# Turning an FFN's hidden features with transposing transfers of 16-bit halves in place of TensorE transposes

## Chip, cores and metric

One Trainium2 chip, one of its cores. The metric is device time in microseconds (us) for one execution of the whole program. TensorE (PE) multiplies, VectorE (DVE) and ScalarE (ACT) do elementwise work, GpSimd (POOL) here mostly issues accumulating transfers, and SyncE (SP) issues nearly all other transfers.

## The reference, cut to what matters

Float32 throughout, 512 tokens of width 1024. The change lies in the two feed-forward networks (FFN) of the block, which have 2816 hidden features each:

```python
def swiglu(h, w1, w3, w2):
    return (jax.nn.silu(h @ w1) * (h @ w3)) @ w2

x = x + 0.5 * swiglu(rms_norm(x, ffn1_norm[l]), ffn1_w1[l], ffn1_w3[l], ffn1_w2[l])
...                       # two token mixers, merged by gates, and an output projection
x = x + 0.5 * swiglu(rms_norm(x, ffn2_norm[l]), ffn2_w1[l], ffn2_w3[l], ffn2_w2[l])
return rms_norm(x, final_norm)
```

## The kernel before, in words

A float32 product is made of three TensorE products: each operand is split into a high part (a copy on ScalarE) and a low part (a subtraction on VectorE), and `mm3` multiplies high by high, high by low and low by high.

Each FFN runs in three stages. The first 256 hidden features are made in a plain way. The other 2560 are five *wide blocks* of 512 features (class `Wide`, L650). A block is computed with seven products (n = 0 to 6) instead of eight, a Strassen-like scheme over two token halves and two halves of the depth. One product is 24 matmuls of 128x128 by 128x512. The last stage (class `Seven`, `run`, L570 on) multiplies the hidden features by `w2`, again with seven products.

`s.order` (L666 to 670) lists the (block, product) pairs, 35 in all; `blocks` (L898 on) walks it, and `m` is the place in the list. In the middle of the walk, block b-1 is not finished when block b begins: the list reads (b,0), (b-1,3), (b-1,4), (b,1), (b,2), (b,6), (b,5). During product m the weights of product m+2 are split into a ring of four slots, one half when the first 12 matmuls of m are done and one when the other 12 are (`weight`, L705). Behind each split, `weight` issues the next transfer into the buffer it read: plain loads from SP (`plain`, L688), accumulating ones from POOL (`add`, L692). `finish` (L801) takes a product's sum out of PSUM.

A block's result lies in `u`: `u[0]` holds tokens 0 to 255 and is ready after product 4, where VectorE multiplies it by the gate `p`; `u[1]` holds tokens 256 to 511 and is ready after product 3, where it is multiplied by the gate `sa`. Each is 128 tokens x 2 x 512 features. The last stage needs features on the partitions, so the block is turned. `turn_all` (L793) does it for blocks 0 to 3: for each of four 128-feature groups, four 128x128 transposes on TensorE (against `ident`) into one PSUM bank, and one ScalarE copy of 128x512 into `s.seven.hidden(j)`, which are the tiles `rl` and `rh`. Block 4 is turned by `turn` (L783), which is another function.

Inside `blocks`, VectorE, ScalarE and TensorE run in the order in which the code is written (class `Queued`, L92). The order on SP is chosen by the framework's scheduler. ScalarE works through its row in order, so an instruction that waits holds up all casts behind it.

Before the second FFN, `tokens` (L1083) already turns eight other tiles with transposing transfers: ScalarE takes the two 16-bit halves of each float32 apart, SP issues a transfer with `transpose=True` (L1087), and POOL joins the halves (L1089).

Of the kernel before, what the change touches and what calls it, by code (L numbers as in the profile page):

```python
# [12 lines left out]
U16 = mybir.dt.uint16  # L13
# [6 lines left out]
P = 128  # L20
# [62 lines left out]
def kernel(  # L83
# [6 lines left out]
    nc = tc.nc  # L90
# [17 lines left out]
    dve, act, pe = [Queued(e, False) for e in (nc.vector, nc.scalar, nc.tensor)]  # L108
# [22 lines left out]
    ident = cp.tile([P, P], F32, name="ident")  # L131
# [368 lines left out]
    KH, TH, LO, HI = KF // 2, T // 2, slice(0, D // 2), slice(D // 2, D)  # L500

    BLOCKS, EARLY = (KF - 2) // 4, 2
# [147 lines left out]
    class Wide:  # L650


        def __init__(s, hp, kind, nrm, w1, w3, w2, quads, residual, C=None):
            def four(name):
                return [hp.tile([P, 2, T], F32, name=f"{name}{h}")[:] for h in range(2)]

            s.nrm, s.w, s.x, s.residual, s.later = nrm, (w1, w3), quads, residual, ()
            s.seven = sv = kind(hp, w2)
            s.A, s.B, s.C = [four("ca"), four("cd")], four("cb"), C or four("cc")
            s.extra = hp.tile([P, 2, T], F32R, name="extra")  # L660
            s.u = [hp.tile([P, 2, T], F32, name=f"u{i}")[:] for i in range(2)]
            q = [hp.tile([P, 2, 4, TH], F32R, name=f"q{i}") for i in range(3)]
            s.q = {n: (t[:, 0], t[:, 1]) for n, t in zip((1, 4, 3), q)}
            s.small = [hp.tile([P, NB], F32, name=f"sm{n}") for n in range(5)]
            s.end = BLOCKS - 1
            s.order = [(b, n) for n in (0, 6) for b in range(EARLY)]  # L666
            s.order += [(0, 1), (0, 2), (0, 4), (0, 5), (1, 1), (0, 3), (1, 2), (1, 4), (1, 5)]
            for b in range(EARLY, BLOCKS):
                s.order += [(b, 0), (b - 1, 3), (b - 1, 4)][:3 if b > EARLY else 2] + [(b, n) for n in (1, 2, 6, 5)]
            s.order += [(s.end, 4), (s.end, 3)]  # L670
            sv.parts = kind.PARTED
            e, o = [t[:].rearrange("p a t -> p (a t)").rearrange("p (b d) -> p b d", b=2) for t in quads]
            flat = [t.rearrange("p a t -> p (a t)") for t in (*s.C, *s.u)]
            sv.wide, sv.fg = s, flat[2]
            sv.O = [o[:, 0], o[:, 1], flat[0], flat[1]]
            sv.e = [t.rearrange("p (k t) -> p k t", t=TH) for t in (e[:, 0], e[:, 1], flat[3][:, 0:3 * TH])]
            a1, a0 = s.chain(s.end - 1), s.chain(s.end)
            sv.sum = [*a1, *s.B, a0[0], a0[1][:, 0:1]]
# [111 lines left out]
                cols = slice(half * TH, (half + 1) * TH)  # L790
                act.copy(s.seven.hidden(2 + 4 * s.end + f)[:, cols], s.turns[f][:, cols])

        def turn_all(s, b, fs):  # L793
            for f in fs:
                ps = s.Y[b % 2][f % 2]
                for i in range(4):
                    pe.transpose(ps[:, i * P:(i + 1) * P], s.u[i // 2][:, i % 2, f * P:(f + 1) * P], ident[:])
            for f in fs:
                act.copy(s.seven.hidden(2 + 4 * b + f), s.Y[b % 2][f % 2][:])

        def finish(s, m):  # L801
            b, n = s.order[m]
# [95 lines left out]
        def blocks(s, pa, pb, more):  # L898
            sv, end, nrm = s.seven, s.end, s.nrm
            raw = [[t[k][:, 0:TH] for k in range(KD)] for t in (nrm.hi, nrm.lo)]  # L900
            soon = {(0, 0): ((s.sums, 1),), (0, 6): ((s.low, 1),), (1, 6): ((s.low, 2),), (0, 1): ((s.low, 4),),
                    (0, 2): ((s.low, 5),), (0, 5): ((s.low, 3),)}
            todo = {(0, 0): ((s.gated, 0),),
                    (1, 0): ((s.cast, 1), (s.sums, 2)),
                    (0, 6): ((s.cast, 2), (s.sums, 4), (s.back, 0)),
                    (1, 6): ((s.cast, 4), (s.sums, 5), (s.hidden, 1, pa[:], pb[:])),
                    (0, 1): ((s.cast, 5), (s.gated, 1)),
                    (0, 2): ((s.cast, 3),),
                    (0, 5): ((s.cast, 0),),
                    (0, 3): ((s.low, 0), (s.cast, 6)),  # L910
                    (1, 2): ((s.low, 6), *[(s.plain, sv.O[i], s.residual[i]) for i in range(2)]),
                    (2, 5): ((sv.second, 0),), (3, 2): ((sv.two, 0),),
                    (end, 0): ((sv.operand, 0, 0),), (end, 2): ((sv.operand, 0, 1),), (end, 6): ((sv.one, 0),),
                    (end, 5): ((sv.second, 1), (sv.one, 1)), (end, 4): ((sv.two, 1),)}
            for at, steps in more.items():
                todo[at] = tuple(todo.get(at, ())) + steps
            for m, (b, n) in enumerate(s.order):
                apart = n == 4 and (b < EARLY or b == end)
                early = m < 2 * EARLY
                ps = s.X[b % 2] if n in (0, 2, 3, 5) or early else s.X[(b + 1) % 2] if n == 6 or apart else s.Y[b % 2]  # L920
                onto = n in (2, 3, 5) or (n == 6 and early) or (n == 4 and not apart)
                last = m + 2 >= len(s.order)
                if last:
                    sv.slots += s.ring[2 * m % 4:2 * m % 4 + 2]
                for h in range(2):
                    wh, wl = s.ring[(2 * m + h) % 4]
                    for i in range(2):
                        for k in range(2):
                            c = slice(i * P, (i + 1) * P)
                            if early:  # L930
                                qh, ql = [t[4 * (n > 0) + 2 * h + k][:, c] for t in raw]
                            else:
                                qh, ql = [t[:, 2 * h + k, c] for t in s.q[n]]
                            mm3(ps[i][:], qh, ql, wh[:, k], wl[:, k], not onto and h + k == 0, h + k == 2, onto)
                    if b > 1 and (n, h) == (2, 0):
                        s.turn_all(b - 1, (2, 3))
                    if (b, n) == (1, 2):
                        s.turn_all(0, ((0, 1), (2, 3))[h])
                    if h == 1:
                        if m == len(s.order) - 1:  # L940
                            s.turns = dict(zip((0, 2, 1, 3), s.Y[end % 2] + s.X[1 - end % 2]))
                            act.activation(s.sa[0], ps[0][:], AF.Silu)
                            act.activation(s.sa[1], ps[1][:], AF.Silu)
                            s.turn((0, 2), 0)
                            for i in range(2):
                                dve.tensor_tensor(s.u[1][:, i], s.u[1][:, i], s.sa[i], op=ALU.mult)
                            sv.operand(0, 2)
                        else:
                            s.finish(m)
                        if b > 1 and n == 1:  # L950
                            s.turn_all(b - 1, (0, 1))
                    if h == 1:
                        for f, *a in soon.get((b, n), ()):
                            f(*a)
                    if not last:
                        s.weight(m + 2, h)
                    elif len(sv.slots) == 2:
                        sv.weight(0, h)
                    elif h == 0:
                        sv.slots.insert(2, s.last)  # L960
                        sv.weight(0, 2)
                        sv.weight(0, 3)
                    else:
                        sv.weight(0, 4)
                s.gate(m)
                for f, *a in todo.get((b, n), ()):
                    f(*a)
            sv.slots.append(tuple(tmp("g5", (P, 1, T), F32R)[:] for _ in range(2)))
            sv.junk = [tmp(f"osq{i}")[:] for i in range(2)]
            sv.weight(0, 5)  # L970
            sv.run()
# [121 lines left out]
    with ExitStack() as mx:  # L1093
# [102 lines left out]
        for o, c0, mu in ((spare[2], DA, 4), (spare[3], 0, 0)):  # L1196
            ps = bank("pk", pf)
# [3 lines left out]
        for p in range(NP):  # L1201
            za.append((zslots[2 * p], zslots[2 * p + 1]))
            for i, (w_, x_, par0, o) in enumerate(((uw, lw, PAR_W0, zslots[2 * p]), (ux, lx, PAR_A0, zslots[2 * p + 1]))):
                ps = bank("pz", (pr, pf)[i])
# [181 lines left out]
        for t in range(C - 1):  # L1386
            n, m = t + 1, C - 1 - t
# [103 lines left out]
        at = b1.go(range(2))  # L1491
# [9 lines left out]
        at = b1.go(range(2, 5), a0.sum(at))  # L1501
# [3 lines left out]
        at = b1.go(range(5, 7), b0.sum(at))  # L1505
# [16 lines left out]
        at = ahead.go(range(7))  # L1522
# [254 lines left out]
        sees, turned, exps, copies, yb = [], ([], []), [], [], []  # L1777
# [176 lines left out]
        ycs, sqs, pgs, pus, parts = [None] * NP, [None] * NP, [None] * NP, [None] * NP, {}  # L1954
# [70 lines left out]
        ps = proj(0, fox_proj, ybs, fws[0])  # L2025
        for m in range(KD):
# [11 lines left out]
            if m + 1 < KD:  # L2038
                ps = proj(m + 1, fox_proj, ybs, fws[m + 1])
# [29 lines left out]
        for m in range(KD):  # L2069
            g = slot[m]  # L2070
            ps = proj(m, rwkv_proj, ya)
# [136 lines left out]
```

## Time and profile before

| what | value |
|---|---|
| median of 3 runs | 1082.54 us (1082.31 to 1082.6) |
| the profiled execution's own time | 1083.12 us |
| its span | 1081.3 us |
| granted TensorE clock | 0.999 |
| instructions | 16859 |

The profile has a page (busy time of each engine, 40 slices of the span, the chain that ended last, groups of instructions) and views on its trace: a timeline of single instructions, busy times in chosen stretches, and waits. A row of the timeline gives start, duration, engine, line, operation, output <- inputs, and in brackets the idle time before it with what ended it. Matmuls overlap: a matmul of 128x512 has a duration of 0.39 us, and the next one starts 0.23 us later, so the pace on TensorE is read from starts, not from durations. Line L103 is the recording helper through which most instructions of the FFN go, so there the names of the tiles tell them apart. The names are: `P` a PSUM bank; `swhi`, `swlo`, `sraw`, `extra` the ring of split weights; `ca`, `cb`, `cc`, `cd` the buffers in which weights land; `u`, `p`, `sa` as above. In this profile, the wide blocks of the first FFN run until about 231 us, those of the second from about 770 to 968 us.

### The profile page before, as it was taken

How to read it: one execution, taken by the hardware profiler on the slowest of the kernel's cores; microseconds unless marked ns; L12 is line 12 of the kernel's file. 1: busy time of each engine (PE TensorE's matmuls, PEld its weight loads, DVE VectorE, ACT ScalarE, POOL GpSimd, SP SyncE). 2: the span in 40 equal slices, each digit the busy share in tenths (PEclk: the TensorE clock that was granted, in tenths of full speed). 3: DMA queues.
4: the chain of work that ended last, by engine and by line, in shares of the span. 5: the costliest groups of instructions: out<-in, count | busy, mean ns of one | idle time of the engine just before them, and what ended most of it. 6: DMA issues, size and time to landing. Idle time of an engine off the chain costs nothing.

```text
span 1081.3 us, 16859 instructions
## 1 busy us (share of the span) xinstructions
PE 1072.1 (99%) x6346; PEld 881.2 (81%) x6346; DVE 829.7 (77%) x1155; ACT 677.4 (63%) x1063; POOL 223.9 (21%) x275
## 2 busy tenths in 40 slices
PE   9999999999999999999999999999999999999997
PEld 7888888888887887888878887888888888888886
DVE  7998575789865698888777777866697666699874
ACT  6775556576555666445888876545576555576554
POOL 1221120134202302412000120125321212114210
PEclk9999999999999999999999999999999999999999
DMA  7989978769955443444312244677977979869972
GB/s 209 261 174 229 217 164 207 180 150 187 233 138 167 110 115 95 128 136 118 89 46 81 91 133 148 192 161 205 290 156 178 211 197 188 194 147 203 235 189 78
DMA packets 150543, 179.23 MB, mean 166 GB/s; under 512 B 20542, under 2 KB 86654, under 8 KB 150462
## 3 DMA queue, kind: packets, MB, share of 16 engines
q0 software_dynamic: 33392, 70.14, 33.8%
q1 hardware_dynamic: 116334, 106.58, 33.1%
q10 hardware_dynamic: 736, 1.45, 0.3%
q8 instruction: 50, 0.82, 0.3%
q14 instruction: 31, 0.25, 0.1%
HBM read 163.51 MB, written 12.52 MB: 163 GB/s over the span
## 4 chain that ended last, share of the span: by engine, by line
PE 96%; DVE 2%; ACT 1%; issue 1%; DMA 0%; ACTq 0%; DVEq 0%
PE P L103 40%; PE P L176 6%; PE P L175 6%; PE P L177 6%; PE pgt L103 5%; PE l L103 3%; PE spot L103 3%; PE pq L103 3%; PE ppj L103 2%; PE pk L177 2%; PE pk L175 2%; PE pk L176 2%; PE pw L176 1%; PE pw L177 1%; PE pw L175 1%; PE f L103 1%
## 5 line engine op out<-in xcount | busy, mean ns | idle before, releaser
L103 PE MATMUL P<-sraw,q 128*128 128x512 f32 x344 | 91.3, 389 | 0.0
L103 PEld LDWEIGHTS P<-sraw,q 128*128 128x128 f32 x344 | 64.6, 188 | 13.4
L103 PE MATMUL P<-swhi,q 128*128 128x512 f32 x224 | 71.4, 390 | 0.0
L103 PE MATMUL P<-sraw,wxh 128*128 128x512 f32 x200 | 68.4, 394 | 0.0
L167 ACT CAST whi<-raw 128x1024 fp32r<-128x1024 f32 (+2 forms) x42 | 40.4, 961 | 43.3 <-issue 14.2
L103 PE MATMUL P<-swhi,wxh 128*128 128x512 f32 x144 | 56.9, 395 | 0.0
L103 PE MATMUL P<-swhi,wxl 128*128 128x512 f32 x144 | 56.1, 390 | 0.0
L103 PE MATMUL P<-swlo,wxh 128*128 128x512 f32 x144 | 56.1, 389 | 0.0
L168 DVE TENSOR_TENSOR wlo<-raw,whi 128x1024 fp32r<-128x1024 f32 (+2 forms) x43 | 48.5, 1127 | 9.4 <-ACT whi L167 8.3
L693 POOL DMA_DIRECT2D cd<-in_ffn_w_dram x24 | 29.5, 1229 | 119.2 <-DVE swlo L103 38.3
L693 POOL DMA_DIRECT2D cb<-in_ffn_w_dram x20 | 24.1, 1207 | 144.7 <-DVE cd L103 80.0
L103 PE MATMUL P<-sraw,wxl 128*128 128x512 f32 x136 | 53.0, 390 | 0.0
L103 PEld LDWEIGHTS P<-swhi,q 128*128 128x128 f32 x224 | 42.1, 188 | 8.7
L103 PE MATMUL P<-swlo,q 128*128 128x512 f32 x112 | 43.6, 389 | 0.0
L103 ACT CAST sraw<-cd 128x1024 fp32r<-128x1024 f32 x30 | 31.5, 1050 | 19.0 <-PE P L103 11.5
L103 ACT COPY RD<-spot 32x128 f32<-32x128 f32 (+2 forms) x128 | 39.9, 311 | 5.3 <-PE spot L103 2.3
L103 PEld LDWEIGHTS P<-sraw,wxh 128*128 128x128 f32 x200 | 37.2, 188 | 7.3
L552 POOL DMA_DIRECT2D ca<-in_ffn_w_dram x16 | 19.3, 1205 | 95.8 <-DVE swlo L103 66.5
L103 DVE TENSOR_TENSOR u<-P,u 128x512 f32<-128x512 f32 x52 | 34.1, 684 | 5.8 <-ACT u L103 5.6
L103 DVE TENSOR_TENSOR swlo<-cc,swhi 128x1024 fp32r<-128x1024 f32 x20 | 24.5, 1225 | 18.2 <-ACT swhi L103 17.9
L177 PE MATMUL pk<-xh,wlo 128*128 128x512 f32 x96 | 37.5, 392 | 1.0 <-DVE wlo L168 1.0
L175 PE MATMUL pk<-xh,whi 128*128 128x512 f32 x96 | 38.0, 396 | 0.4 <-DVE u L1241 0.4
(626 smaller groups left out, 3434.4 us busy)
## 6 DMA issues: line engine op xcount, KB each, us to landing
raw<-in_w_in_dram SPq DMA_DIRECT2D x40, 512.0 KB
cc<-in_ffn_w_dram SPq DMA_DIRECT2D x36, 512.0 KB
cb<-in_ffn_w_dram POOLq DMA_DIRECT2D x36, 512.0 KB, 6.1
cb<-in_ffn_w_dram SPq DMA_DIRECT2D x32, 512.0 KB
cd<-in_ffn_w_dram POOLq DMA_DIRECT2D x32, 512.0 KB, 7.4
ca<-in_ffn_w_dram POOLq DMA_DIRECT2D x32, 512.0 KB, 7.3
ca<-in_ffn_w_dram SPq DMA_DIRECT2D x20, 512.0 KB
cd<-in_ffn_w_dram SPq DMA_DIRECT2D x18, 512.0 KB
```

The costliest lines, as they stand in the source:

```text
L103: q.last = do(*a, **kw)
L167: (hi_eng or act).copy(hi[:], raw[:])
L168: (eng or dve).tensor_tensor(lo[:], raw[:], hi[:].bitcast(F32), op=ALU.subtract)
L175: pe.matmul(ps, whi, xhi, start=first, stop=False, skip_group_check=onto)
L176: pe.matmul(ps, whi, xlo, start=False, stop=False, skip_group_check=onto)
L177: return pe.matmul(ps, wlo, xhi, start=False, stop=last, skip_group_check=onto)
L552: nc.gpsimd.dma_start(s.sum[g], src, accum_op=ALU.add)
L693: nc.gpsimd.dma_start(to, s.block(b, n, h), accum_op=ALU.add)
```

## The change

`turn_all` and its calls are gone. In its place, for blocks 0 to 3 of both FFNs:

- `apart`, at the end of product 4 (for `u[0]`) and of product 3 (for `u[1]`): for each of the two token groups, ScalarE copies 128x512 float32 as 1024 16-bit numbers, low halves first and then high halves, into the gate tile that has just been used (`p` or `sa`), and SP issues one transposing transfer of 128x1024 16-bit numbers back into the place in `u` that they came from.
- `joined`, three products later, behind the split of the first half of weights: four ScalarE copies of 128x512 16-bit numbers, which put the halves together again in `hidden(j)`.

And `s.order` has (b-1,4) ahead of (b-1,3) from block 3 on, as it had already at the end of the list.

```diff
-                s.order += [(b, 0), (b - 1, 3), (b - 1, 4)][:3 if b > EARLY else 2] + [(b, n) for n in (1, 2, 6, 5)]
+                s.order += [(b, 0)] + [(b - 1, 4)] * (b > EARLY) + [(b - 1, 3)] + [(b, n) for n in (1, 2, 6, 5)]
...
-        def turn_all(s, b, fs):
-            for f in fs:
-                ps = s.Y[b % 2][f % 2]
-                for i in range(4):
-                    pe.transpose(ps[:, i * P:(i + 1) * P], s.u[i // 2][:, i % 2, f * P:(f + 1) * P], ident[:])
-            for f in fs:
-                act.copy(s.seven.hidden(2 + 4 * b + f), s.Y[b % 2][f % 2][:])
+        def apart(s, b, half):
+            for i in range(2):
+                parts = (s.sa if half else s.p[b])[i].bitcast(U16)
+                act.copy(parts.rearrange("p (s c) -> p c s", s=2), s.u[half][:, i].bitcast(U16).rearrange("p (c s) -> p c s", s=2))
+                nc.sync.dma_start(s.u[half][:, i].bitcast(U16).rearrange("p (a t) -> p a t", t=P), parts, transpose=True)
+
+        def joined(s, b, half):
+            turned = s.u[half].rearrange("p i t -> p (i t)").bitcast(U16).rearrange("p (i s f t) -> p f i t s", i=2, s=2, t=P)
+            for f in range(4):
+                to = s.seven.hidden(2 + 4 * b + f)[:, half * TH:(half + 1) * TH].bitcast(U16)
+                act.copy(to.rearrange("p (i t s) -> p i t s", i=2, s=2), turned[:, f])
...
-                    if b > 1 and (n, h) == (2, 0):
-                        s.turn_all(b - 1, (2, 3))
-                    if (b, n) == (1, 2):
-                        s.turn_all(0, ((0, 1), (2, 3))[h])
...
-                        if b > 1 and n == 1:
-                            s.turn_all(b - 1, (0, 1))
...
+                    for at, half, b_ in joins:
+                        if (m, h) == (at, 0):
+                            s.joined(b_, half)
+                if n in (3, 4) and b < end:
+                    s.apart(b, int(n == 3))
+                    joins.append((m + 3, int(n == 3), b))
```

On TensorE the 64 rows of two transposes each go, and blocks 2 and 3 change the order of two products; nothing else moves there. From the first FFN's end to the second's beginning the rows of all engines read as before, but for line and buffer numbers.

The first place is ScalarE in the first FFN, at the end of block 1's product 4, where the list of products is densest. `p_503`, `p_504` are the gate tiles of block 1, `u_384` is `u[0]`, `u_385` is `u[1]`, which still holds block 0.

```order
 L103 CAST swhi<-cd_379 128x1024
 L103 CAST swhi<-cd_380 128x1024
+L103 COPY p_503<-u_384 128x512x2
+L103 COPY p_504<-u_384 128x512x2
 L103 CAST sraw<-ca_377 128x1024
+L103 COPY rl_371<-u_385 128x512
+L103 COPY rh_374<-u_385 128x512
+L103 COPY rl_371<-u_385 128x512
+L103 COPY rh_374<-u_385 128x512
 L103 COPY u_385<-P_497 128x512
 L103 COPY u_385<-P_498 128x512
```

The two copies that take block 1's first half apart and the four that join block 0's second half stand here close behind each other, ahead of the copies that take the next sum out of PSUM into `u[1]`.

The second place is ScalarE in the first FFN, at the end of block 3's products 4 and 3. `P_497`, `P_498` hold the sum of product 3, and the casts write the ring's slots.

```order
 L103 CAST swhi<-cd_379 128x1024
+L103 CAST swhi<-cd_380 128x1024
+L103 COPY p_503<-u_384 128x512x2
+L103 COPY p_504<-u_384 128x512x2
+L103 CAST sraw<-cd_379 128x1024
 L103 ACTIVATE sa_455<-P_497 128x512
 L103 ACTIVATE sa_456<-P_498 128x512
-L103 CAST swhi<-cd_380 128x1024
-L103 CAST sraw<-cd_379 128x1024
 L103 CAST sraw<-cd_380 128x1024
+L103 COPY sa_455<-u_385 128x512x2
+L103 COPY sa_456<-u_385 128x512x2
```

Product 4 now ends first, so its half is taken apart a product ahead of the other half, which follows behind the gate's activation.

The third place is SP in the first FFN, at its first transposing transfers (block 0). `cd`, `cc` and `cb` are weight loads.

```order
+L797 DMA_TRANSPOSE u_384<-p_505 128x8x128
+L797 DMA_TRANSPOSE u_384<-p_506 128x8x128
 L690 DMA cd_379<-in_ffn_w_dram 128x2x512
 L690 DMA cd_380<-in_ffn_w_dram 128x2x512
 L690 DMA cc_363<-in_ffn_w_dram 128x2x512
-L690 DMA cc_364<-in_ffn_w_dram 128x2x512
+L797 DMA_TRANSPOSE u_385<-sa_455 128x8x128
+L690 DMA cc_364<-in_ffn_w_dram 128x2x512
+L797 DMA_TRANSPOSE u_385<-sa_456 128x8x128
 L690 DMA cb_381<-in_ffn_w_dram 128x2x512
 L690 DMA cb_382<-in_ffn_w_dram 128x2x512
```

The transposing transfers stand among the loads in SP's one row, each waiting there for its ScalarE copy.

1 line of the change is left out of this document (added).

## Prediction

> **What bounds the kernel now.** I read the page first: busy times, slices, chain.
>
> ```profile
> PE 1072.1 (99%) x6346; PEld 881.2 (81%) x6346; DVE 829.7 (77%) x1155; ACT 677.4 (63%) x1063; POOL 223.9 (21%) x275
> ...
> PE   9999999999999999999999999999999999999997
> ...
> DMA  7989978769955443444312244677977979869972
> ...
> PE 96%; DVE 2%; ACT 1%; issue 1%; DMA 0%; ACTq 0%; DVEq 0%
> ```
>
> TensorE is busy in every slice and makes up 96% of the chain that ended last: what it issues is the time, and whatever leaves it is gained if nothing else comes late. The second reading is how near the others are in the stretches of the wide blocks (columns: busy us of each engine with instructions, clock, share of the DMA engines, GB/s).
>
> ```profile
> core 0: us, PE busy (x) PEld busy (x) DVE busy (x) ACT busy (x) POOL busy (x), PEclk, DMA share, GB/s
> 35.00:75.00 40.00, 40.00 (x178) 33.14 (x177) 38.88 (x44) 28.54 (x35) 8.68 (x8) 1.00 0.91 207
> 155.00:195.00 40.00, 40.00 (x186) 33.32 (x185) 27.62 (x29) 22.99 (x30) 7.26 (x6) 1.00 0.82 185
> 195.00:235.00 40.00, 40.00 (x191) 33.29 (x190) 31.94 (x35) 25.74 (x35) 7.36 (x7) 1.00 0.72 167
> 235.00:275.00 40.00, 40.00 (x182) 33.15 (x181) 37.62 (x40) 25.50 (x32) 17.15 (x15) 1.00 1.08 191
> 895.00:935.00 40.00, 40.00 (x186) 33.31 (x185) 27.63 (x29) 23.11 (x30) 7.36 (x7) 1.00 0.82 184
> ```
>
> Where blocks are turned (about 90 to 207 us, and again in the second FFN), ScalarE is busy 23 of 40 us and VectorE 28. VectorE is nearly full only ahead of that (35 to 75) and behind it (235 to 275).
>
> **What TensorE loses.** The group of these transposes, and the timeline around one call's eight of them:
>
> ```profile
> L103 PE MATMUL P<-ident,u 128*128 128x128 f32 x160 | 21.3, 272 | 0.0
> ...
> 90.06 0.39 PE L103 MATMUL P<-sraw,wxl 128*128 128x512 f32 x1
> 90.30 1.03 PE L103 MATMUL P<-ident,u 128*128 128x128 f32 x8
> 91.08 0.48 PE L103 MATMUL P<-sraw,wxh 128*128 128x512 f32 x1
> 91.40 0.39 PE L103 MATMUL P<-extra,wxh 128*128 128x512 f32 x1
> ...
> 209.10 0.39 PE L103 MATMUL P<-swhi,wxh 128*128 128x512 f32 x1
> ...
> 211.82 0.39 PE L103 MATMUL P<-swhi,wxh 128*128 128x512 f32 x1
> ...
> 214.54 0.62 PE L103 MATMUL P<-sraw,wxh 128*128 128x512 f32 x2
> ```
>
> The last three rows are a product's beginning, its middle and the next one's beginning: 24 matmuls in 5.44 us, 0.227 us each. From 90.06 to 91.40 lie two matmul steps (0.45 us) and eight transposes: 1.34 - 0.45 = 0.89 us for eight. Of the 160 transposes, `turn` keeps 32 (16 in each FFN), so 128 go, 16 groups of eight: 16 x 0.89 = 14.2 us, all on the path.
>
> **What ScalarE gets.** Prices come from these groups:
>
> ```profile
> L103 ACT COPY rh<-P 128x512 f32<-128x512 f32 x16 | 9.5, 593 | 0.0
> ...
> L103 ACT CAST swhi<-cc 128x1024 fp32r<-128x1024 f32 x20 | 21.1, 1054 | 14.9 <-PE P L103 11.2 <-issue 3.7
> ...
> L1086 ACT COPY G<-xS 128x512 uint16<-128x512 uint16 x12 | 6.7, 610 | 0.0
> ```
>
> Per block, four copies of 0.59 us out of PSUM go (2.4 us). Eight joining copies of 512 16-bit numbers come, at the 0.61 us of L1086 (4.9 us), and four copies that take 1024 numbers apart. No row shows one that writes 16-bit numbers 1 KB apart in turn: the near rows are the cast of as many numbers (1.05 us) and two of L1086 (1.22). I take 1.1, and keep twice that, 2.2, as the upper end; I see no reason for less than the cast. That is 4.4 us, and 6.9 us net per block. A block's seven products take 38.1 us, ScalarE's busy time goes from about 23 to 30 of them: it fits on average. What counts is where the copies stand. A cast has this cover (ScalarE, then VectorE, in block 3 to 4; used by the row at 211.82 above):
>
> ```profile
> 203.48 1.06 ACT L103 CAST swhi<-cc 128x1024 fp32r<-128x1024 f32 x1
> ...
> 204.57 1.23 DVE L103 TENSOR_TENSOR swlo<-cc,swhi 128x1024 fp32r<-128x1024 f32 x1 [2.86 <-ACT swhi L103]
> ```
>
> The slot is whole at 205.80 and used at 211.82, 6.0 us later, so some 4.4 us of copies can push in ahead of a cast at no cost. The worst place is the first order piece of the change, where six copies (2 x 1.1 + 4 x 0.61 = 4.6 us) stand in about one product:
>
> ```profile
> 106.37 1.05 ACT L103 CAST sraw<-ca 128x1024 fp32r<-128x1024 f32 x1
> ...
> 107.46 1.23 DVE L103 TENSOR_TENSOR extra<-ca,sraw 128x1024 fp32r<-128x1024 f32 x1 [0.26 <-ACT sraw L103]
> ...
> 114.08 0.39 PE L103 MATMUL P<-extra,q 128*128 128x512 f32 x1
> ...
> 114.02 1.05 ACT L103 CAST swhi<-cd 128x1024 fp32r<-128x1024 f32 x1 [2.04 <-DMA cd<-in_ffn_w_dram]
> ```
>
> The slot made from the cast at 106.37 is whole at 108.69 and needed at 114.08, which moves to 112.3 (two groups of transposes lie ahead of it): 3.6 us of cover against 4.6 us, less what idle time ahead of the cast absorbs. The cast at 114.02 already waits 2 us for an accumulating transfer. I put 0.5 us of TensorE waiting here, in each FFN; between nothing and 2.
>
> **The transfers.** The nearest rows are the transposing ones of the same size between the FFNs, on SP, with the POOL copy that waits for them:
>
> ```profile
> 728.78 1.84 SPq L1087 DMA_TRANSPOSE G<-G  x1
> ...
> 733.50 2.18 POOL L1089 COPY G<-G 128x512 uint16<-128x512 uint16 x2 [0.92 <-DMA G<-G]
> ...
> 755.17 1.88 SPq L690 DMA_DIRECT2D cb<-in_ffn_w_dram  x2
> 757.62 8.51 SPq L1087 DMA_TRANSPOSE rh<-rh  x1
> 766.24 4.48 SPq L1087 DMA_TRANSPOSE rl<-rl  x1
> ...
> 775.05 2.84 POOL L1089 COPY rl<-rl 128x512 uint16<-128x512 uint16 x2 [0.24 <-DMA rl<-rl]
> ```
>
> Quiet, one lands 4.7 us after its issue began and holds SP 1.84 us, so a pair has landed after 6.6 us. With loads queued ahead on SP, the last pair took from 757.62 to 775.05: 17.4 us. These are the ends. When is it needed? Let T be the end of product 4, where VectorE's rows begin:
>
> ```profile
> 196.73 1.28 DVE L103 TENSOR_TENSOR u<-P,u 128x512 f32<-128x512 f32 x2
> 197.93 1.28 DVE L103 TENSOR_TENSOR u<-u,p 128x512 f32<-128x512 f32 x2
> ```
>
> The first token group is done at T + 1.8, taken apart by T + 3, and there the first issue begins. ScalarE comes to the joining copies behind a cast that waits for two and a half products: T + 13.6 + 1.05 = T + 14.7, 11.7 us after the issue. A later landing costs ScalarE first: four joins (2.4), the next cast (1.05) and its subtraction (1.23) have to be done by T + 24.5, when TensorE uses that slot (it is freed at T + 16.3, and used 8.2 later). So TensorE waits only if the pair lands later than 24.5 - 4.7 = T + 19.8, 16.8 us after the issue. The stretches that hold the pairs have a DMA share of 0.72 to 0.82, nearer to the quiet rows; I take 8 to 12 us, no wait on average, and 1 us in all for a single late pair.
>
> The Trainium skill (VectorE: DVE Perf Modes, The three transpose paths) gives 390 ns for a 128x128 bf16 transpose on TensorE and 1309 ns for one by a transposing DMA, and its rules take TensorE where the result may go to PSUM; the 256 16-bit squares here would by an estimate from that page be 335 us of transfers, against 305 us of products in eight blocks: a loss of at least 30 us where I have a gain. The trace disagrees: eight squares land together within 4.7 us.
>
> **What shares SP's row.** 32 issues of 1.8 us hold SP, and loads stand behind them (the third order piece):
>
> ```profile
> 105.78 3.31 SPq L690 DMA_DIRECT2D ca<-in_ffn_w_dram  x2
> ...
> 132.16 1.05 ACT L103 CAST swhi<-ca 128x1024 fp32r<-128x1024 f32 x1 [1.19 <-PE P L103]
> ...
> 122.23 4.10 SPq L690 DMA_DIRECT2D cc<-in_ffn_w_dram  x2
> ...
> 143.20 1.05 ACT L103 CAST swhi<-cc 128x1024 fp32r<-128x1024 f32 x1 [1.23 <-issue]
> ```
>
> The load `ca` will stand behind block 1's first pair and be late by up to two issues, 3.7 us; it is issued 26 us ahead of its use. POOL's row reads the same before and after. The load `cc` at 122.23 feeds block 2's product 4, which now comes one product earlier: 21.0 - 5.4 = 15.5 us remain. The exchange of products 3 and 4 thus costs nothing as long as loads land within that; nor does VectorE do more than before. VectorE's dense stretch behind the blocks starts from the same state, since it waits for ScalarE just ahead of it (2.86 us at 204.57).
>
> **Sum.** The profiled execution took 1083.12 us (1081.3 us of span and 1.8 around it), 0.58 above the median of 1082.54. 1083.12 - 14.2 + 1.0 (dense place) + 1.0 (late pair) = 1070.9; less 0.6 for the median: 1070.3 us.
>
> **Rivals.**
>
> *Slower: pairs land late and hold ScalarE.* For it: SP's queue carries weight loads, and the loaded pair took 17.4 us. A block's second pair is issued about a product behind the first on the same queue; if it had to wait its turn as `rl` did (8.8 us from issue to landing behind a pair that needed 17.4), it would land 17.4 - 5.4 + 8.8 = 20.8 us after its issue. TensorE would then wait 17.4 - 16.8 = 0.6 and 20.8 - 16.8 = 4.0 us per block: 4.6 x 8 = 37 us, and 1083.1 - 14.2 + 37 + 1 = 1106.9, 1106 on the median's scale. It turns from gain to loss at 14.2 / 8 = 1.8 us of TensorE waiting per block. Against it: ten loads of 512 KB had been issued in the 6.6 us ahead of that pair, while a product of a wide block issues two at most. Chance 0.14. (This is also the outcome to which the page's 1309 ns would lead.)
>
> *The copies on 16-bit halves cost twice their rows.* Four times 1.1 and eight times 0.61 more, 9.3 us per block: ScalarE would be busy 39 of 38.1 us and be the bound there, by about 1 us per block, and the dense place would wait 4 us more in each FFN: 1070.9 + 8 x 1 + 8 = 1086.9 at most, and with half of that taken by the cover 1078.9, 1078 on the median's scale. Against it: the 16-bit row stands at 0.61 beside 0.59 for float32. Chance 0.10, at 1078.
>
> *No gain: the change takes the transposes off TensorE and another engine keeps the pace.* It would need VectorE or the loads to bound the stretches with transposes; VectorE's 28 of 40 us speak against it. Loads late by some of the 16-engine time that transfers add could eat it: 1082. Chance 0.06.
>
> **How the numbers follow.** The forecast, 1067.5 to 1075, has 0.70; the dear copies 0.10; no gain 0.06; slower 0.14. About 0.2% (2.2 us) is what a measurement of this kernel can tell from no change. Faster: 0.70 + 0.10 - 0.01 = 0.79; same 0.06; slower 0.15. The floor is 14.2 us off with no wait at all, 1068.3, less a little for a group's mean: 1067.5. The upper end takes in the dear copies and most of the no-gain case: 1082.
>
> **What would show it.** In the profile after, the `ident,u` group on TensorE has 32 rows, and TensorE's matmuls start 5.44 us per product with no wait between; the `COPY p<-u` and `COPY sa<-u` rows last about 1.1 us, the joins about 0.6; `rl<-u` waits little or nothing for the DMA. I am wrong if joins wait over 5 us for `u`, if TensorE shows idle time ahead of `swhi`, `sraw` or `extra`, or if casts wait for `cc` or `cd`.

## The result and the profile after

The changed kernel takes 1182.34 us (median of 4 runs, 1181.43 to 1182.95), the kernel before 1082.57 beside it: 1.092 times as long, with a 95% interval of 1.0902 to 1.0940. The forecast was 1070.3, and its range ended at 1082. From the page after, the busy times and the slices of TensorE and of its clock:

```profile
span 1181.2 us, 16755 instructions
...
PE 1101.9 (93%) x6218; PEld 889.6 (75%) x6218; DVE 829.9 (70%) x1155; ACT 841.4 (71%) x1127; POOL 223.3 (19%) x275
...
PE   9988787979999999999999999999987797889997
...
PEclk9998888989999999999999999999989798989999
```

TensorE has lost its full row of nines in two places, the two FFNs' wide blocks. Its idle time went from 1081.3 - 1072.1 = 9.2 us to 1181.2 - 1101.9 = 79.3. Its busy time rose too, although its transposes went: 1072.1 - 14.2 = 1057.9 was to be expected, and 1101.9 is 44 us more. The mean granted clock of the run is 0.960, and 1057.9 / 0.960 = 1102.0. So 70 us are waits, and 44 us are the same matmuls at a lower granted clock. The clock falls with the waits: each of the 16 waits of TensorE that last over 2 us has a stretch of 3.4 or 6.8 us at 0.50 (92 us in all), which begins within the wait or up to some 2 us after it. Single microseconds of the first such place, in the wait, behind it and later (the third number from the end is the clock):

```profile
82.00:83.00 1.00, 0.00 (x0) 0.00 (x0) 0.00 (x0) 1.00 (x1) 0.00 (x0) 1.00 1.11 201
87.00:88.00 1.00, 1.00 (x2) 0.29 (x1) 1.00 (x3) 1.00 (x2) 0.00 (x0) 0.50 0.68 126
95.00:96.00 1.00, 1.00 (x6) 0.82 (x5) 1.00 (x1) 1.00 (x2) 0.00 (x0) 1.00 1.06 172
```

ScalarE is 164 us busier. Its groups on 16-bit numbers (which the kernel before has not), and the waits of TensorE:

```profile
L103 ACT COPY p<-u 128x1024 uint16<-128x1024 uint16 x16 | 76.0, 5008 | 14.3 <-DVE u L103 14.3
L103 ACT COPY sa<-u 128x1024 uint16<-128x1024 uint16 x16 | 75.7, 4984 | 0.0
L103 ACT COPY rh<-u 128x512 uint16<-128x512 uint16 x32 | 21.7, 679 | 0.0
```

```profile
PE P L103 <- ACT u L103: 28.8, 6, 7.4
PE P L103 <- ACT swhi L103: 17.4, 6, 3.8
PE P L103 <- ACT sraw L103: 12.2, 4, 3.8
```

Each of the 32 copies that take a tile apart lasts 5.0 us where 1.1 was taken: 32 x 3.9 = 125 us of ScalarE. TensorE, which waited for ScalarE nowhere in the wide blocks, now waits for it three times over: for the copies out of PSUM (`u`) and for the casts (`swhi`, `sraw`). No join waits for a transfer. The same place shows how it goes (timeline at block 0's product 4; start, duration, and in brackets the idle time ahead):

```profile
75.67 9.44 ACT L103 COPY p<-u 128x1024 uint16<-128x1024 uint16 x2
...
80.59 5.77 SPq L797 DMA_TRANSPOSE u<-p  x2
...
84.62 1.34 ACT L103 CAST swhi<-cd 128x1024 fp32r<-128x1024 f32 x1
85.86 1.05 ACT L103 COPY u<-P 128x512 f32<-128x512 f32 x2
...
86.49 0.80 PE L103 MATMUL P<-swhi,q 128*128 128x512 f32 x1 [4.89 <-ACT u L103]
```

Two copies hold ScalarE for 9.44 us; the cast and the copies out of PSUM that stand behind them come late, and TensorE stops for 4.9 us. The matmul behind the gap takes 0.80 us, twice the 0.39 of the others. By stretches (busy us with instructions, clock, DMA share, GB/s), where the kernel before has TensorE at 40.00 and clock 1.00:

```profile
75.00:115.00 40.00, 30.13 (x111) 22.91 (x110) 19.19 (x20) 36.02 (x27) 3.65 (x3) 0.86 0.68 144
155.00:195.00 40.00, 36.92 (x150) 29.60 (x149) 23.79 (x27) 29.39 (x26) 6.36 (x6) 0.93 0.74 171
```

### The profile page after: what moved, and what is told of

It reads as the page before. It is cut to its first block, busy times and chain, and to the rows that moved or that the text cites. A ratio compares the mean times of both kernels' runs of the same rounds, so it can differ in the third digit from the quotient of the medians.

```text
span 1181.2 us, 16755 instructions
## 1 busy us (share of the span) xinstructions
PE 1101.9 (93%) x6218; PEld 889.6 (75%) x6218; DVE 829.9 (70%) x1155; ACT 841.4 (71%) x1127; POOL 223.3 (19%) x275
## 5 line engine op out<-in xcount | busy, mean ns | idle before, releaser
L103 PE MATMUL P<-sraw,wxh 128*128 128x512 f32 x200 | 79.7, 449 | 21.5 <-ACT sraw L103 12.2
L103 PEld LDWEIGHTS P<-sraw,q 128*128 128x128 f32 x344 | 66.7, 194 | 28.5 <-ACT u L103 14.4
L103 ACT COPY p<-u 128x1024 uint16<-128x1024 uint16 x16 | 76.0, 5008 | 14.3 <-DVE u L103 14.3
L103 PE MATMUL P<-swhi,q 128*128 128x512 f32 x224 | 75.1, 407 | 11.7 <-ACT u L103 8.5
L103 PE MATMUL P<-swhi,wxh 128*128 128x512 f32 x144 | 63.0, 438 | 17.4 <-ACT swhi L103 17.4
L103 ACT COPY sa<-u 128x1024 uint16<-128x1024 uint16 x16 | 75.7, 4984 | 0.0
L167 ACT CAST whi<-raw 128x1024 fp32r<-128x1024 f32 (+2 forms) x42 | 40.4, 961 | 43.1 <-issue 14.2
L103 PEld LDWEIGHTS P<-sraw,wxh 128*128 128x128 f32 x200 | 43.1, 216 | 36.2 <-ACT sraw L103 13.9
L103 PE MATMUL P<-swlo,wxh 128*128 128x512 f32 x144 | 62.5, 434 | 3.5 <-DVE swlo L103 3.5
L103 PE MATMUL P<-swhi,wxl 128*128 128x512 f32 x144 | 61.4, 426 | 0.0
L103 PEld LDWEIGHTS P<-swhi,wxh 128*128 128x128 f32 x144 | 30.5, 212 | 26.5 <-ACT swhi L103 20.0
L103 DVE TENSOR_TENSOR swlo<-cd,swhi 128x1024 fp32r<-128x1024 f32 x24 | 29.3, 1221 | 19.3 <-ACT swhi L103 19.3
L103 DVE TENSOR_TENSOR swlo<-ca,swhi 128x1024 fp32r<-128x1024 f32 x20 | 24.4, 1222 | 25.4 <-ACT swhi L103 25.4
```

Of the source, the lines that this page charges most:

```text
L103: q.last = do(*a, **kw)
L167: (hi_eng or act).copy(hi[:], raw[:])
```

## The experiments

Below, the cheap order is the changed kernel with one line of `apart` written the other way round: first all low halves, then all high ones, so that the writes run straight and the reads take every second number. The expectations name three theories: W, that the copy's order of writing is the cause; T, that the transfers are; E, that any 16-bit copy of this size is dear. From "A later join" on, every changed kernel keeps the cheap order; the pieces by themselves are put into the kernel before.

### The order of writing alone

```diff
-act.copy(parts.rearrange("p (s c) -> p c s", s=2), s.u[half][:, i].bitcast(U16).rearrange("p (c s) -> p c s", s=2))
+act.copy(parts.rearrange("p (s c) -> p s c", s=2), s.u[half][:, i].bitcast(U16).rearrange("p (c s) -> p s c", s=2))
```

> The copy that takes the halves apart keeps its data, but walks them in the other order: all low halves, written one behind the other, then all high halves (it reads every second 16-bit number). Theory W (the 5.0 us are the price of writing 16-bit numbers in turn to two places 1 KB apart): this copy lasts 1.0 to 1.3 us, ScalarE loses about 120 us of busy time, and the time falls to the forecast, 1068 to 1075 us. Theory T (the transfers: pairs that land late, loads that stand behind them): the time stays above 1090 us whatever this copy costs. Theory E (any 16-bit copy of 1024 numbers out of u costs 5 us): the copy stays at 4 to 5 us and the time at 1170 to 1185.

Measured: 1094.66 us (1092.07 to 1098.48), 1.0115 times before (1.0088 to 1.0142). The copies fall from 5.0 to 1.05 us, and with them go 87.7 us of the 99.8 that were lost: E is out. But the time is above the 1068 to 1075 of W, and still slower than before, so T holds in part. ScalarE's waits now name the transfers:

```profile
ACT rl L103 <- DMA u<-sa: 21.6, 4, 7.0
ACT swhi L103 <- DMA cc<-in_ffn_w_dram: 18.1, 2, 9.6
...
ACT swhi L103 <- DMA cd<-in_ffn_w_dram: 9.5, 3, 4.6
```

### The transfers away, with either order

Both leave out the 32 transposing transfers, so the features are joined unturned. The copies and joins stay, but the joins read straight, and one of them lasts 0.62 us instead of 0.68. First with the change's order, then with the cheap one.

```diff
-                nc.sync.dma_start(s.u[half][:, i].bitcast(U16).rearrange("p (a t) -> p a t", t=P), parts, transpose=True)
...
-            turned = s.u[half].rearrange("p i t -> p (i t)").bitcast(U16).rearrange("p (i s f t) -> p f i t s", i=2, s=2, t=P)
+            turned = s.u[half].rearrange("p i t -> p (i t)").bitcast(U16).rearrange("p (i f t s) -> p f i t s", i=2, s=2, t=P)
```

> The change as it is, without its 32 transposing transfers (the joining copies read the block unturned, so the features are not turned). W: ScalarE still makes the 32 copies of 5.0 us, so the time stays at 1170 to 1185 us. T: without the transfers it falls below 1095 us.

> The cheap order of the copy, and no transposing transfers (features not turned). If the transfers cost nothing, within 2 us of the run with the cheap order and its transfers. If late pairs or the loads behind them cost something there, that much faster, 3 us or more.

Measured: 1179.66 and 1072.54 us (one run each). With the two runs above this makes a square of four:

| copies write | with transfers | without | the transfers cost |
|---|---|---|---|
| in turn (the change) | 1182.34 | 1179.66 | 2.7 |
| straight (cheap order) | 1094.66 | 1072.54 | 22.1 |
| the order costs | 87.7 | 107.1 | |

The change's loss comes apart as 1072.54 - 1082.5 = -10.0 for the transposes off TensorE, +107.1 for the order of writing, +2.7 for the transfers: 99.8 us. With the change's order no join waits for a transfer, and the transfers cost next to nothing; we take it that the slow copies make everything behind them late anyway. With the cheap order the same transfers cost 22, to within some 3 us, since the four runs of the cheap order spread over 6 us and the kernels without transfers ran once. The transfers' row includes 64 joins that are 0.06 us dearer.

### The copy by itself

Eleven ways to copy, three times each, put at the start of the kernel before; the total isn't compared.

```diff
...
+nc.scalar.copy(d16.rearrange("p (s c) -> p c s", s=2), tick)
+nc.scalar.copy(d16.rearrange("p (s c) -> p s c", s=2), tock)
...
```

> The kernel before, with eleven copies of one 128x512 float32 tile added at its start, three times each; its time is not compared. They measure the disputed copy by itself. W: on ScalarE 1024 16-bit numbers written in turn to two places 1 KB apart last 4.9 to 5.1 us, in straight order 1.1. If distance matters (two places 256 or 32 bytes apart), the near ones are cheaper, 1 to 3 us; if only the turn matters they are 5 us as well. If the width matters, 512 float32 numbers written in turn to two places last 0.6 us; if each write that does not follow the last costs the same, 2.5 us. If leaving one 16-bit place free is enough, 512 numbers written to every second place last 2.5 us, else 0.6. If it is ScalarE's, VectorE and GpSimd take no longer for the turn than for the straight order; if it is the memory's, they too take over twice as long.

The rows (least, median and greatest ns; L314 has the change's order, L315 the cheap one, L317 has two places 256 bytes apart; L321 and L322 are the first two on VectorE, L323 and L324 on GpSimd):

```profile
L314 ACT COPY mbd<-mbs x3: 4737/4837/4922, 2.8 to 88.6; 128x1024 uint16<-128x1024 uint16 x3
L315 ACT COPY mbd<-mbs x3: 1038/1042/1047, 7.6 to 93.6; 128x1024 uint16<-128x1024 uint16 x3
L316 ACT COPY mbd<-mbs x3: 4802/4831/4862, 8.9 to 94.6; 128x1024 uint16<-128x1024 uint16 x3
L317 ACT COPY mbd<-mbs x3: 4682/4699/4752, 14.0 to 99.5; 128x1024 uint16<-128x1024 uint16 x3
L318 ACT COPY mbd<-mbs x3: 1076/1096/1130, 20.2 to 104.2; 128x512 f32<-128x512 f32 x3
L319 ACT COPY mbd<-mbs x3: 753/759/762, 22.6 to 105.3; 128x512 uint16<-128x512 uint16 x3
L320 ACT COPY mbd<-mbs x3: 1156/1167/1169, 24.8 to 106.1; 128x1024 uint16<-128x1024 uint16 x3
L321 DVE COPY mbd<-mbs x3: 2734/2804/2965, 25.9 to 107.3; 128x1024 uint16<-128x1024 uint16 x3
L322 DVE COPY mbd<-mbs x3: 675/695/715, 29.1 to 110.1; 128x1024 uint16<-128x1024 uint16 x3
L323 POOL COPY mbd<-mbs x3: 4687/5107/7937, 30.0 to 110.9; 128x1024 uint16<-128x1024 uint16 x3
L324 POOL COPY mbd<-mbs x3: 1042/1042/1520, 35.2 to 115.7; 128x1024 uint16<-128x1024 uint16 x3
```

Writing 16-bit numbers in turn to two places costs 4.84 us, straight 1.04; two places 32 or 256 bytes apart (L316, L317) cost about the same as 1 KB. The same order on float32 (L318) costs 1.10 for 512 numbers, against 0.59 straight in the rows of before. Every second 16-bit place in one row (L319) costs 0.76, and reading in turn from two places 1 KB apart while writing straight (L320) 1.17. VectorE pays 2.80 against 0.70 and GpSimd 5.11 against 1.04, so it is no matter of ScalarE alone. What is dear is the writing that changes its place with every number, and it is dear for 16-bit numbers above all: 4.7 ns a number, against 2.1 for float32. These rows don't separate what the change of place costs from what writing half a word costs.

### Where the 22 us of the transfers come from

In the cheap order's run, SyncE's row at blocks 2 and 3, and ScalarE's rows there:

```profile
152.58 3.29 SPq L797 DMA_TRANSPOSE u<-p  x2
157.42 9.23 SPq L797 DMA_TRANSPOSE u<-sa  x2
...
198.64 8.48 SPq L797 DMA_TRANSPOSE u<-sa  x2
207.22 1.69 SPq L690 DMA_DIRECT2D cc<-in_ffn_w_dram  x2
```

```profile
175.96 0.68 ACT L103 COPY rl<-u 128x512 uint16<-128x512 uint16 x1 [7.04 <-DMA u<-sa]
...
217.41 1.04 ACT L103 CAST swhi<-cc 128x1024 fp32r<-128x1024 f32 x1 [8.42 <-DMA cc<-in_ffn_w_dram]
```

The first half's pair is joined without a wait in this run. The second half's pair, issued five microseconds later, lands 175.96 - 157.42 = 18.5 us after its issue began, holds SyncE for 9 us instead of 3, and the load of `cc` behind it comes 8 us late (block 3). That is what reaches TensorE: VectorE's subtraction waits for this cast, the row of VectorE behind it (`p<-P,p`) frees the PSUM bank late, and TensorE stops twice, once in each FFN, for 9.8 us in all:

```profile
PE P L103 <- DVE p L103: 9.8, 2, 5.5
...
220.46 0.77 PE L103 MATMUL P<-swhi,q 128*128 128x512 f32 x1 [4.29 <-DVE p L103]
```

Between the profiled executions with and without transfers TensorE's idle time differs by 15.1 us (26.8 against 11.7) and its busy time by 7.4 (1066.3 against 1058.9); with each of the two stops the clock stands at 0.50 for 6.8 us.

The transfers' packets (counted in the microsecond in which they start) show what the second pair of block 2 meets:

```
us     adding loads, KB   transposing, KB
156           0                226
161         188                  3
162         178                 16
163         106                 46
167          45                 21
170          39                 22
173          90                 39
174          35                 95
```

Alone, either kind moves about 200 KB per us (161 and 156). A transposing packet has 256 bytes, an adding one 2 KB: at 162 the engines take 61 and 87 of them, at 163 already 180 and 52. From 164 to 171 both crawl, and single packets are slow: an adding one takes 0.18 us at 161 and 0.74 at 170. In the stretches (the last two numbers are the DMA share and GB/s) this is a full share that moves little:

```profile
160.00:163.00 3.00, 3.00 (x15) 2.49 (x14) 1.78 (x2) 1.33 (x2) 0.00 (x0) 1.00 1.12 192
165.00:174.00 9.00, 9.00 (x41) 7.46 (x40) 4.70 (x5) 3.88 (x6) 1.20 (x1) 1.00 1.42 80
```

The Trainium skill (DMA: Bandwidth & Descriptors, Queues, rings and completion order) has each engine go round the queues packet by packet; the counts at 162 come near to that, those at 163 and 167 (83 and 22) do not, and the crawl no rule there gives.

**A later join.** The second half of blocks 1 to 3 joined one product later.

```diff
-joins.append((m + 3, int(n == 3), b))
+joins.append((m + 3 + (n == 3 and b > 0), int(n == 3), b))
```

> The cheap copy order, with the second token half of blocks 1 to 3 joined one product later (5.4 us). Theory 'collision' (the second half's pair of transposing transfers is slow because it is in flight together with the accumulating loads; what it then costs is the waits in which it ends): ScalarE's wait for u<-sa, 21.6 us in four places in the run with the cheap order, falls below 6 us (7.0 us a place less 5.4); the casts still wait for cc and cd, whose loads stand behind the pair on SP (27.6 us in five places there), and the time is 1083 to 1092 us against 1094.7. Rival 'queue' (the joins wait because ScalarE meets them too early, the casts' lateness follows only from the joins' wait): both waits go, 1072 to 1078 us. Rival 'load' (all DMA engines full, everything late alike): no change, 1092 to 1096.

Measured: 1098.43 us (1097.38 to 1102.14), above all three expectations. The wait for `u<-sa` is gone from ScalarE's list, as 'collision' had it, but the time has not come back: the casts' wait for `cc` grew.

```profile
ACT swhi L103 <- DMA cc<-in_ffn_w_dram: 29.9, 6, 11.0
```

So the join's wait was not what cost; by the waits, the loads behind the held pair on SyncE were.

**Plain loads in place of adding ones.** Same sizes, places and queue; the sums of the weights are left out.

```diff
-nc.gpsimd.dma_start(to, s.block(b, n, h), accum_op=ALU.add)
+nc.gpsimd.dma_start(to, s.block(b, n, h))
```

> The cheap copy order, all transfers in place; the accumulating loads of the wide blocks are plain loads of the same size, places and queue (the weights' sums are left out, so the output is another). Theory 'collision' in its strict form (it is the adding that slows the transposing): the second half's pair lands as soon as the first half's, ScalarE's wait for u<-sa falls from 21.6 to under 4 us, waits for cc and cd under 8, time 1070 to 1076 us. Rival 'queue or load' (any load of that size beside the pair does it): both waits stay, 1088 to 1096 us. One reservation: a plain load may itself be quicker than an adding one, so the issue-to-landing times beside the waits decide between them.

Measured: 1071.82 us (one run), and neither `u<-sa` nor `cc` is left among ScalarE's larger waits. All transfers are in place here, and they cost nothing that shows: 1071.8 beside the 1072.5 without them. So it is not the transfers' bytes, nor their place behind the loads on SyncE; it takes the adding loads of this kernel beside them. The reservation in the expectation holds: a plain load is also quicker, and this run does not tell whether it is the adding itself or the longer time that such loads take.

**The pair beside loads, by itself.** At the end of the kernel before, with the other engines idle. A first such piece (its parts ran into each other, so that it does not price them) still shows the crawl:

> The kernel before with a piece at its end, twice: a pair of transposing transfers alone, the same pair beside four accumulating loads of 512 KB, beside four plain loads on the same queue, beside four plain loads on another queue, and the four accumulating loads alone. Theory 'collision': the pair alone lands in 6 to 8 us after the first issue, beside plain loads in up to 12, beside accumulating loads in over 16, and those loads take longer than alone. Rival 'load': plain and accumulating loads delay the pair alike. The total time isn't compared.

```profile
1145.00:1151.00 6.00, 0.00 (x0) 0.00 (x0) 0.00 (x0) 0.00 (x0) 0.75 (x1) 0.50 2.37 43
1178.00:1186.00 8.00, 0.00 (x0) 0.00 (x0) 0.69 (x6) 0.00 (x0) 1.20 (x1) 0.50 1.11 199
```

43 GB/s at a share of 2.37, where adding loads, plain ones and the pair were in flight together, against 199 for adding loads alone, and TensorE and ScalarE idle: the crawl lies among the transfers themselves. A second piece holds the parts apart:

> The kernel before with a piece at its end, twice, each part of it begun when the one ahead has landed: the pair of transposing transfers alone; four adding loads of 512 KB alone, and with the pair; four plain loads on the same queue alone, and with the pair; four plain loads on ScalarE's queue alone, and with the pair. Theory 'by turns' (a DMA engine that serves both queues takes one packet of each in turn; a transposing packet has 256 bytes, a load's 2 to 4 KB): the pair beside any loads moves about 25 KB per us while they last against about 240 alone, so it lands with or after the loads; adding loads (near 200 KB per us alone) last about 10 us, plain ones half as long, so the pair lands 12 to 17 us after its issue beside adding loads and 7 to 10 beside plain ones. Rival 'adding alone': beside plain loads it lands as if alone, within 7 us. The total time isn't compared.

VectorE's rows mark the start of each part (L2216) and the landings (L2220 the two transfers of the pair, L2222 the loads):

```profile
1083.57 0.37 DVE L2216 COPY mba<-mbk 128x2 f32<-128x2 f32 x4
...
1088.30 0.17 DVE L2220 CAST mbk<-mbt 128x2 f32<-128x2 uint16 x1 [1.02 <-DMA mbt<-mbs]
...
1104.28 0.37 DVE L2216 COPY mba<-mbk 128x2 f32<-128x2 f32 x4
...
1107.59 0.37 DVE L2220 CAST mbk<-mbt 128x2 f32<-128x2 uint16 x1 [2.94 <-DMA mbt<-mbs]
1113.82 0.17 DVE L2220 CAST mbk<-mbt 128x2 f32<-128x2 uint16 x1 [5.87 <-DMA mbt<-mbs]
...
1120.99 0.17 DVE L2222 COPY mbk<-mba 128x2 f32<-128x2 f32 x1 [2.37 <-DMA mba<-in_ffn_w_dram]
...
1131.00 0.37 DVE L2216 COPY mba<-mbk 128x2 f32<-128x2 f32 x4
...
1136.39 0.17 DVE L2220 CAST mbk<-mbt 128x2 f32<-128x2 uint16 x1 [5.02 <-DMA mbt<-mbs]
1143.50 0.17 DVE L2220 CAST mbk<-mbt 128x2 f32<-128x2 uint16 x1 [6.94 <-DMA mbt<-mbs]
```

The pair lands after 4.7 us alone, 9.5 beside four adding loads, 12.5 beside four plain ones, and 12.0 beside plain ones on ScalarE's queue; the second pass gives 4.9, 9.7, 12.6 and 12.1. Four adding loads take 14.4 us alone and 16.7 with the pair, four plain ones 9.3 and at most 12.5. Both expectations fail: any load delays the pair two or three times over ('adding alone' is wrong), and the plain ones delay it more, not less ('by turns' had it the other way). The two are not quite alike, though: the pair's first transfer lands 3.3 us after the start beside adding loads, as soon as alone (3.5), for their first packet starts only 2.8 us after it; beside plain ones it lands after 5.4. The second transfer takes 6.2 and 7.1 us more. Nothing here crawls as at 165 us.

**Another time for the late pairs.** The second half is taken apart and sent one product later in block 1, two in blocks 2 and 3, and joined one later.

```diff
+                if n == 3 and b < end:
+                    late.append((m + min(b, 2), b))
+                    joins.append((m + 3 + (b > 0), 1, b))
...
+                for at, b_ in late:
+                    if m == at:
+                        s.apart(b_, 1)
```

> The cheap copy order, both token halves by transfers, but the second half's copies and pair of transfers come later: one product later for block 1, two for blocks 2 and 3, where the run with half the transfers shows the adding queue empty (about 128 to 133 and 168 to 175 us); they are joined one product later than before. Block 0 stays as it was. Theory 'collision in time' (the pair crawls only while adding loads are in flight): the pairs land in 4 to 7 us after their issue, ScalarE's wait for u<-sa is under 6 us in all, and so are the casts' waits for cc that the cheap order brought; nearly all of TensorE's gain is left, 1070.5 to 1075 us, below the 1076.45 of half the transfers. Rival 'bytes' (the transfers are too much for the DMA engines wherever they stand): the loads behind the pair on SP come late instead, cc and cb waits of over 10 us and 1080 to 1090 us.

Measured: 1081.68 us in the median, but from 1077.86 to 1090.28 over ten runs, no difference from before (0.9973 to 1.0020). In the profiled run (1077.96) the pairs land in time, no wait for `u<-sa` or `cc` stands among the larger ones, and the stretch that crawled moves 289 GB/s:

```profile
165.00:175.00 10.00, 10.00 (x46) 8.29 (x45) 6.46 (x7) 8.45 (x11) 1.95 (x2) 1.00 1.10 289
```

So in this run the time of the pair decides whether it is late, as expected. The total is not as expected: even the fastest run lies above the 1070.5 to 1075 of 'collision in time', the spread between runs of one kernel was foreseen by neither theory, and no trace shows a slow one.

**Half the transfers.** Only the first half goes by transfers; the second is turned by TensorE as in the kernel before.

```diff
+def turn_half(s, b):
+    spots = [s.Y[b % 2][f // 2][:, f % 2 * TH:(f % 2 + 1) * TH] for f in range(4)]
+    for f in range(4):
+        for i in range(2):
+            pe.transpose(spots[f][:, i * P:(i + 1) * P], s.u[1][:, i, f * P:(f + 1) * P], ident[:])
+    for f in range(4):
+        act.copy(s.seven.hidden(2 + 4 * b + f)[:, TH:], spots[f])
...
+if n == 4 and b < end:
+    s.apart(b, 0)
...
```

> The cheap copy order, and only the first token half is turned by transfers; the second half is turned by TensorE as before (64 transposes and their PSUM copies stay). Theory 'collision': the first half's pair was never late in the run with the cheap order, and what was late (second half's pair, 21.6 us of ScalarE's wait, and the cc and cd loads behind it on SP) has no cause left: 8 groups of eight transposes at 0.89 us are saved, 1082.5 - 7.1 = 1075.4, 1073.5 to 1077.5 us, ScalarE's wait for u<-sa gone and waits for cc and cd as in the kernel before. Rival 'load' (the DMA engines are full in these stretches and half as many transfers still push the loads late): half of the 22 us that the transfers cost stay, 1082 to 1086.

Measured: 1076.45 us (1076.21 to 1076.84), 0.9942 times before (0.9926 to 0.9959): it beats both kernels, and steadily, where 'collision' expected it (1073.5 to 1077.5). TensorE keeps 96 of its 160 transposes, and its stretch that had the waits is full but for 0.2 us:

```profile
L103 PE MATMUL P<-ident,u 128*128 128x128 f32 x96 | 13.6, 274 | 0.4 <-DVE u L103 0.4
```

```profile
195.00:235.00 40.00, 39.79 (x188) 32.68 (x187) 31.61 (x35) 28.96 (x45) 7.80 (x7) 1.00 0.77 180
```

**And block 0's second half too.**

```diff
-if n == 4 and b < end:
+if b < end and (n == 4 or (b, n) == (0, 3)):
...
```

> As the run with half the transfers (1076.45 us), and block 0's second half goes by transfers too: in the run with the cheap order its pair was issued at 90.9 and 94 us, between two stretches of adding loads, and nothing waited for it. Theory 'collision in time': two more groups of eight transposes go (one in each FFN), 2 x 0.89 = 1.8 us less, 1074.0 to 1075.5. Rival 'bytes': each further pair costs the loads behind it what it saves, 1076 to 1078. The difference is about the smallest that can be measured here.

Measured: 1080.4 us in the median of twelve runs, from 1075.30 to 1086.52 (0.9957 to 1.0000 times before). The fastest runs come near to where 'collision in time' put them, 1.2 us under the run before this one; the median lies above both expectations. One pair more in each FFN is enough to bring back the spread.

## Why the prediction was wrong

**The copies apart: the step that failed.** "No row shows one that writes 16-bit numbers 1 KB apart in turn ... I take 1.1, and keep twice that, 2.2, as the upper end" measured 5.0. Both near rows write straight; the order of writing was what was new in the operation, and it was given no price of its own. The rival 'copies on 16-bit halves cost twice their rows' had, at 0.10, the right effect (dear copies make ScalarE the bound), but with a factor of 2 where it was 4.5, and for another reason: 16-bit copies that write straight cost 1.05. With 5.0 and 0.68 its own sum gives 4 x 5.0 + 8 x 0.68 - 2.4 = 23.0 us more of ScalarE per block, 46 in the 36.3 us of seven products without transposes, about 10 us per block or 78 in all; measured, without the transfers, were 107.1, of which 66.0 are TensorE's idle time (77.7 us with the change's order, 11.7 with the cheap one) and 41.1 its busy time (1100.0 and 1058.9). For the clock that falls with the waits neither the sum nor the rival has a term. The Trainium skill bears on it (Advanced Engine Details and Errata, Memory Cachelines): SBUF has lines of 16 bytes, and an access that goes to another line each time is penalized. It gives no figure, and the prediction did not weigh it. The rows agree for writing (two places 32 bytes apart cost as much as 1 KB), hardly for reading in turn (1.17 against 1.04).

**TensorE's 14.2 us** were nearly right: with cheap copies and no transfers 10.0 us were gained, and plain loads beside the transfers leave 10.8. Of the 4.2 us that are missing, 1.0 is TensorE's busy time, which falls by 13.2 (1072.1 to 1058.9), and 2.5 are waits (11.7 us idle instead of 9.2) that lie outside the wide blocks, most of them between the two FFNs; why is not shown. In the dense place, for which 1.0 was taken, TensorE waits under 0.1. The joins cost 0.68 instead of 0.61.

**The transfers: "8 to 12 us, no wait on average"** held in the changed kernel as to the wait, behind slow copies (2.7 us in all). With cheap copies the second half's pair took 18.5 us, within the 17.4 and 20.8 that the rival 'pairs land late' worked from, and it cost 22 us rather than its 37, as far as the later join shows by the load behind the pair and not, as the rival had it, by the late joins. The reason against that rival, two loads per product against ten, missed what counted: not how many loads stand ahead on SyncE, but adding loads on the other queue while the pair is in flight. The DMA share of 0.72 to 0.82, by which the quiet end was chosen, is a mean over 40 us and does not show where in it the adding loads lie.

**"The load `cc` ... 15.5 us remain"** failed with the cheap order: a cast waited up to 9.6 us for it, since the pair ahead held SyncE for 9 us, not 2 x 1.84.

**VectorE's busy time and POOL's order** stood as predicted (829.7 to 829.9 us). Of the signs named, TensorE's waits for `swhi` and `sraw` came true, and the copies at 4.5 times 1.1; the joins' wait for `u` and the casts' for `cc` appeared only when the copies were cheap.

What stays open: why the pair and the adding loads crawl together in some stretches (80 and 43 GB/s) and merely share in others (both in 16.7 us); what part the adding itself has in it; and the spread of the two kernels with more late pairs.

## What to carry to other kernels

An operation whose pattern of writing is new has no price in rows of the same size: measure it alone, or write it so that the writes run straight and the reads take the steps, which here made 5.0 us into 1.05. Before transfers are put beside others, look at what is in flight in the very microseconds, not at the mean share of the stretch, and at what is queued behind them on their issuer. Where transfers are given to a kernel with slow copies, a second fault can hide behind the first: change each alone and both together to see them (2.7 against 22.1 us for the same transfers).

## What the runs showed of the hardware

- Writing 16-bit numbers in turn to two places: ScalarE 4.84 us for 1024 against 1.04 straight, VectorE 2.80 against 0.70, GpSimd 5.11 against 1.04; on ScalarE much the same at 32 bytes, 256 bytes and 1 KB (4.83, 4.70, 4.84).
- A pair of transposing transfers lands in 4.7 us alone and in 9.5 to 12.5 beside loads on another queue; beside adding loads the DMA engines can fall to 43 to 80 GB/s at a full share.
- TensorE's waits cost twice: with each of the 16 waits of over 2 us the granted clock stood at 0.50 for 3.4 or 6.8 us, and at a mean clock of 0.960 the same matmuls took 44 us more. No threshold follows from the runs: waits of 2.1 and 2.9 us (another time for the late pairs, a later join) had no such stretch, one of 1.3 us (block 0's second half too) had.
